# Within-chunk decays of an SSD scan on Trainium2: ten-row matmuls of split running sums in place of masked 128-row matmuls

## The chip, the cores and the metric

The kernel runs as one program on one core of a Trainium2 chip. The metric is the device time of one execution in microseconds (us). The core has a matrix engine (TensorE, in the profile PE; its weight loads are shown apart as PEld), a vector engine (VectorE, DVE), a scalar engine (ScalarE, ACT), GpSimd (POOL) and SyncE (SP). Each runs its own instructions in a fixed order; semaphores make one engine wait for another. Matmuls write to PSUM, a small memory of banks of 128 x 512 fp32 numbers; everything else stands in SBUF, both with 128 partitions.

## The reference, cut to what matters

The network has two layers on 512 latent tokens (and 256 context tokens) of width 1024. The change is in layer 0, in the Mamba-2 state-space scan (SSD) with 16 heads of width 64 in 2 groups, run once forward and once backward (d = 0, 1), in chunks of 128 tokens:

```python
def ssd_scan(xs, dt, a_coef, bm, cm, h0):
    xdt = (xs * dt[..., None])
    a = dt * a_coef                          # a_coef < 0, per head
    a_cum = jnp.cumsum(a, -1)                # within a chunk
    decay = jnp.exp(segsum(a))               # exp(a_cum[t] - a_cum[s]) for s <= t, else 0
    cb = jnp.einsum('bclgn,bcsgn->bgcls', cc, bc)
    y_diag = jnp.einsum('bgcls,bgjcls,bcsgjp->bclgjp', cb, decay, xdt)
    # ... plus what comes over from earlier chunks (y_off), by exp(a_cum)
```

So for each of 4 chunks, 16 heads and both directions a 128 x 128 table of exponents is needed, which for source token s and target token t holds the difference of two running sums; its exponential, times dt of the source and times `cb`, is the weight with which the source's 64 values go into the target's output. The forward tables are zero for s > t, the backward ones for s < t. A skip term adds `ssd_d` times the input.

## The kernel before, in words

`mixer` (L350 ff.) projects layer 0's input. PE does the projections with weights split in a high and a low fp32r part: per block of 128 input channels three matmuls (L214 to L216) of 512 columns (latents, tile `ps`) or 256 (context, also `ps`). A weight block comes from memory as `wraw`, is cast on ScalarE to `whi` (L184), and VectorE or POOL makes `wlo` as the difference (L188). Few such blocks are in SBUF at a time, so a cast also waits until PE has finished with an older block. The results of a projection for the SSD go through a five-tap convolution, `conv5`: ScalarE does the middle tap from PSUM (L332), VectorE adds four taps, also from PSUM (L336), ScalarE applies silu (L339); PE transposes the result (L347, `pt`) and ScalarE copies it out (L348). The projections' PSUM pool `mm` has four banks; a fifth projection waits until the taps of the first have read its bank. Pools `lv` and `mi` have two banks each.

`dt_stage` (L512) computes dt and a = -dt x exp(a_log) for all chunks, heads and directions (VectorE, up to L552), then with six matmuls `p` (L560 to L562) against triangles of ones the running sums and totals; ScalarE takes their exponentials, `ef` and `dtot` (L565, L566), which free the two `mi` banks, and VectorE makes `wdec`.

`ssd` (L592) is called for the two groups of 8 heads, g = 0 and 1. It makes the states that chunks hand on (matmuls `u`, L620 to L624 and L675) and `pcb`, the products of B and C for four chunks (L629); two VectorE products give `cbm`, masked for forward and backward (L633). Then for each of 4 chunks and for each half `hq` of the group's heads (four heads; 16 such half-chunks in both groups):

- ScalarE multiplies a triangle of ones by `a`, per head and direction: 8 tiles `r` of 128 x 128 (L644)
- PE multiplies these with the strict triangle, one fp32 matmul `seg` of 512 columns a direction, both accumulated in one `lv` bank (L645): the exponents of both directions, each zero where the other counts
- ScalarE takes the exponential to `e` (L647, the one reader of the bank)
- ScalarE and VectorE make `w`, the masked `cbm` times dt of either direction (L650, L651, four each)
- VectorE multiplies `e` by `w` (L653), and PE uses each head's part as the stationary operand of a matmul `yp` (L656).

After each chunk come the two inter-chunk terms `po` (L661), the skip product and the sums on VectorE (L663 to L671, the last is `y` times the gate `sz`) and a square on ScalarE with a running sum (L672).

Between these, PE works on the next weight matmuls: for g = 0 on group 1's projections, for g = 1 on the `v` projection of the gla heads that come next (tile `psv`, copied out by ScalarE at L496) and on the first gla gates (`ps`, L697). The first matmul of a gla head that depends on all of this is `lev` (L733). The order on each engine isn't that of the source: the build lays the whole program out by its dependencies, and the result is a fixed list for each engine.

Of the kernel before, what the change touches and what calls it, by code (L numbers as in the profile page):

```python
# [8 lines left out]
F32 = mybir.dt.float32  # L9
F32R = mybir.dt.float32r  # L10
BF16 = mybir.dt.bfloat16
I32 = mybir.dt.int32
AF = mybir.ActivationFunctionType
ALU = mybir.AluOpType
# [3 lines left out]
P = 128  # L18
D = 1024
KT = D // P  # L20
T = 512
TC = 256
NCH = T // P
# [115 lines left out]
def ap(t, off, dims):  # L139
    a = t[:]  # L140
    return bass.AP(tensor=a.tensor, offset=a.offset + off, ap=[list(a.ap[0])] + [list(d) for d in dims])
# [6 lines left out]
class Net:  # L148
# [201 lines left out]
    def mixer(self):  # L350
# [93 lines left out]
        sp = ss.enter_context(self.pool("ssp", 1))  # L444
        dx = self.stack()
# [3 lines left out]
        dt, a, ef, dtot, wdec = dts  # L449
        self.dump("dt", dt)  # L450
# [61 lines left out]
    def dt_stage(self, act, actc, sp, sx, mm, mi, rows):  # L512
# [51 lines left out]
        dtot = sp.tile([P, 2, NC6, H], F32, name="dtot")  # L564
        nc.scalar.activation(out=ef, in_=p1, func=AF.Exp)  # L565
# [6 lines left out]
        return dt, a, ef, dtot, wdec  # L572
# [19 lines left out]
    def ssd(self, g, y, xct, bfm, cfm, btok, dts, rows, sz, sp, tmps, lv, mi):  # L592
        nc = self.nc
        dt, a, ef, dtot, wdec = dts
# [4 lines left out]
        def bch(t, n):  # L599
            return bass.AP(tensor=t.tensor, offset=t.offset, ap=[list(t.ap[0]), [1, t.shape[1]], [0, n]])  # L600
# [29 lines left out]
        cbm = sp.tile([P, 2, NCH, P], F32, tag="cbm", name="cbm")  # L630
        for d in range(2):
            m = (self.le, self.ge)[d]
            nc.vector.tensor_tensor(out=cbm[:, d], in0=pcb, in1=bass.AP(tensor=m.tensor, offset=m.offset, ap=[list(m.ap[0]), [0, NCH], [1, P]]), op=ALU.mult)  # L633
        ssq = tmps.tile([P, NCH], F32, tag="ssq", name="ssq")
        for c in range(NCH):
            yp = mi.tile([P, 512], F32, tag="mi", name="yp")
            for hq in range(2):
                h0 = g * GH + hq * 4
                r = tmps.tile([P, 2, 4, P], F32, tag="r", name="r", bufs=1)
                seg = lv.tile([P, 4, P], F32, tag="lv", name="seg")  # L640
                for d in range(2):
                    m = (self.le, self.ge)[d]
                    for j in range(4):
                        nc.scalar.mul(r[:, d, j, :], m, a[:, c, d, h0 + j:h0 + j + 1])  # L644
                    nc.tensor.matmul(seg, (self.gt, self.lt)[d], r[:, d], start=d == 0, stop=d == 1)  # L645
                e = tmps.tile([P, 4, P], F32, tag="e", name="e")
                nc.scalar.activation(out=e, in_=seg, func=AF.Exp)  # L647
                w = tmps.tile([P, 4, P], F32, tag="w", name="w")
                for j in range(4):
                    nc.scalar.mul(w[:, j, :], cbm[:, 1, c, :], dt[:, c, 1, h0 + j:h0 + j + 1])  # L650
                    nc.vector.scalar_tensor_tensor(out=w[:, j, :], in0=cbm[:, 0, c, :], scalar=dt[:, c, 0, h0 + j:h0 + j + 1],  # L651
                                                   in1=w[:, j, :], op0=ALU.mult, op1=ALU.add)
                nc.vector.tensor_tensor(out=e, in0=e, in1=w, op=ALU.mult)  # L653
                for j in range(4):
                    hh = hq * 4 + j
                    nc.tensor.matmul(yp[:, hh * HD:(hh + 1) * HD], e[:, j, :], y[:, c, (g * GH + hh) * HD:(g * GH + hh + 1) * HD], start=True, stop=True)  # L656
# [9 lines left out]
            dd = rows[:, R_D - R_DTB + g * GH:R_D - R_DTB + (g + 1) * GH]  # L666
            nc.vector.tensor_tensor(out=heads(yc), in0=heads(yc), in1=bch(dd, HD), op=ALU.mult)
# [577 lines left out]
def layout(inp):  # L1245
# [25 lines left out]
    out["tri"] = np.concatenate([(s == t), (s <= t), (s >= t), (s > t), (s < t)], 1).astype(np.float32)  # L1271
    out["msk"] = np.concatenate([((s // m) ^ (t // m)) == 1 for m in (1, 2, 4, 8, 16, 32, 64)], 1).astype(np.int32)
# [16 lines left out]
```

## Time and profile before

| | us |
|---|---|
| median of 3 runs | 1736.62 |
| lowest, highest | 1735.19, 1737.04 |
| the profiled execution | 1734.44 |
| its span, first to last instruction | 1732.7 |
| PE busy in it | 1696.8 |
| DVE busy | 1220.2 |
| ACT busy | 849.9 |
| POOL busy | 520.0 |

The profile is of one execution. In its rows a line such as `L645 PE MATMUL seg<-r,tri 128x512 x64` names the line of the code, the engine, the operation, the tile written and those read, the form and the count; an fp32 matmul counts as two records. `[0.46 <-DVE y L671]` behind a row is idle time of the engine ahead of it and what ended it. The mean granted clock of TensorE was 0.994 of the full one.

### The profile page before, as it was taken

How to read it: one execution, taken by the hardware profiler on the slowest of the kernel's cores; microseconds unless marked ns; L12 is line 12 of the kernel's file. 1: busy time of each engine (PE TensorE's matmuls, PEld its weight loads, DVE VectorE, ACT ScalarE, POOL GpSimd, SP SyncE). 2: the span in 40 equal slices, each digit the busy share in tenths (PEclk: the TensorE clock that was granted, in tenths of full speed). 3: DMA queues.
4: the chain of work that ended last, by engine and by line, in shares of the span. 5: the costliest groups of instructions: out<-in, count | busy, mean ns of one | idle time of the engine just before them, and what ended most of it. 6: DMA issues, size and time to landing. Idle time of an engine off the chain costs nothing.

```text
span 1732.7 us, 26538 instructions
## 1 busy us (share of the span) xinstructions
PE 1696.8 (98%) x9574; PEld 1458.9 (84%) x9574; DVE 1220.2 (70%) x2416; ACT 849.9 (49%) x1718; POOL 520.0 (30%) x434
## 2 busy tenths in 40 slices
PE   7999999999999999999999999999999999999997
PEld 5987778989999898898888888988899888888886
DVE  7778987979696894768777741378887876666114
ACT  4556775344444553365333332499635743333223
POOL 4400000000000000545444454533424444444443
PEclk9999999999999999999999999999999999999998
DMA  9721002444344233834334343422213333333332
GB/s 362 244 73 50 29 22 90 135 145 147 132 150 139 92 122 102 263 92 130 109 109 121 109 134 97 113 77 55 62 31 86 97 93 97 97 98 97 98 98 79
DMA packets 92195, 194.03 MB, mean 112 GB/s; under 512 B 10496, under 2 KB 13568, under 8 KB 92064
## 3 DMA queue, kind: packets, MB, share of 16 engines
q1 hardware_dynamic: 92016, 192.21, 36.2%
q8 instruction: 75, 1.23, 0.3%
q14 instruction: 56, 0.46, 0.1%
q0 software_dynamic: 48, 0.13, 0.0%
HBM read 190.21 MB, written 2.10 MB: 111 GB/s over the span
## 4 chain that ended last, share of the span: by engine, by line
PE 93%; DVE 3%; ACT 1%; issue 0%; POOL 0%; ACTq 0%; POOLq 0%; DVEq 0%
PE ps L214 18%; PE ps L216 18%; PE ps L215 18%; PE lev L744 3%; PE psg L215 2%; PE psg L216 2%; PE psg L214 2%; PE psh L214 2%; PE psh L215 2%; PE psh L216 2%; PE psz L235 2%; PE psz L234 2%; PE psz L233 2%; PE seg L645 2%; PE psv L234 1%; PE psv L235 1%
## 5 line engine op out<-in xcount | busy, mean ns | idle before, releaser
L188 POOL TENSOR_TENSOR wlo<-wraw,whi 128x512 fp32r<-128x512 f32 x380 | 499.9, 1319 | 1171.7 <-ACT whi L184 1154.7
L184 ACT CAST whi<-wraw 128x512 fp32r<-128x512 f32 x488 | 300.7, 619 | 501.6 <-PE ps L215 249.1
L214 PE MATMUL ps<-h1hi,whi 128*128 128x512 f32 x768 | 299.1, 389 | 0.8 <-DVE acc L1105 0.8
L216 PE MATMUL ps<-h1hi,wlo 128*128 128x512 f32 x768 | 299.0, 389 | 0.2 <-POOL wlo L188 0.2
L215 PE MATMUL ps<-h1lo,whi 128*128 128x512 f32 x768 | 298.9, 389 | 0.0
L1105 DVE SCALAR_TENSOR_TENSOR acc<-ps,pcol,acc 128x441 f32<-128x441 f32 (+2 forms) x320 | 222.4, 695 | 56.9 <-ACT acc L1097 47.4
L214 PEld LDWEIGHTS ps<-h1hi,whi 128*128 128x128 f32 x768 | 144.2, 188 | 30.8 <-issue 1.6
L216 PEld LDWEIGHTS ps<-h1hi,wlo 128*128 128x128 f32 x768 | 144.2, 188 | 30.4 <-POOL wlo L188 0.6
L215 PEld LDWEIGHTS ps<-h1lo,whi 128*128 128x128 f32 x768 | 144.2, 188 | 29.4
L273 DVE CUSTOM_DVE_ANT_0 junk<-ada,sc,pcol 128x1024 bf16<-128x1024 f32 x80 | 106.4, 1330 | 8.7 <-DMA ada<-adaw 8.4
L909 DVE SCALAR_TENSOR_TENSOR x<-ps,mod,x 128x512 f32<-128x512 f32 x14 | 10.5, 750 | 139.0 <-PE ps L216 139.0
L188 DVE TENSOR_TENSOR wlo<-wraw,whi 128x512 fp32r<-128x512 f32 x108 | 73.9, 691 | 42.4 <-ACT whi L184 42.1
L214 PE MATMUL ps<-ghi,whi 128*128 128x512 f32 x264 | 102.7, 389 | 0.0
L215 PE MATMUL ps<-glo,whi 128*128 128x512 f32 x264 | 102.7, 389 | 0.0
L216 PE MATMUL ps<-ghi,wlo 128*128 128x512 f32 x264 | 102.7, 389 | 0.0
L1197 DVE SCALAR_TENSOR_TENSOR cr<-u,pcol,cr 128x511 f32<-128x511 f32 (+20 forms) x156 | 97.9, 702 | 1.4 <-ACT cr L1180 1.2
L214 PE MATMUL ps<-hhi,whi 128*128 128x512 f32 x240 | 97.9, 408 | 0.0
L215 PE MATMUL ps<-hlo,whi 128*128 128x512 f32 x240 | 96.7, 403 | 0.0
L216 PE MATMUL ps<-hhi,wlo 128*128 128x512 f32 x240 | 96.2, 401 | 0.0
L1016 DVE TENSOR_TENSOR glo<-acc,ghi 128x512 fp32r<-128x512 f32 x44 | 56.0, 1273 | 28.2 <-ACT ghi L1015 28.0
L233 PE MATMUL psz<-whi,hhi 128*128 128x256 f32 (+1 forms) x224 | 67.6, 302 | 0.0
L234 PE MATMUL psz<-wlo,hhi 128*128 128x256 f32 (+1 forms) x224 | 67.4, 301 | 0.0
(361 smaller groups left out, 4122.8 us busy)
## 6 DMA issues: line engine op xcount, KB each, us to landing
wraw<-wst SPq DMA_DIRECT2D x488, 256.0 KB, 2.7
ada<-adaw SPq DMA_DIRECT2D x104, 512.0 KB, 3.6
xk<-xT SPq DMA_DIRECT2D x8, 256.0 KB, 7.8
x<-xT SPq DMA_DIRECT2D x8, 256.0 KB, 5.3
out<-n SPq DMA_DIRECT2D x16, 128.0 KB, 1.7
xk<-ctxT SPq DMA_DIRECT2D x8, 128.0 KB, 3.7
sc<-rows SPq DMA_DIRECT2D x1, 512.0 KB, 3.6
scc<-rows SPq DMA_DIRECT2D x1, 512.0 KB, 7.6
```

The lines of the kernel that those rows point to most:

```text
L184: nc.scalar.copy(hi, raw)
L188: eng.tensor_tensor(out=lo, in0=raw, in1=hi.bitcast(F32), op=ALU.subtract)
L214: mm(ps, w[0], a[0], start=start, stop=False)
L215: mm(ps, w[0], a[1], start=False, stop=False)
L216: mm(ps, w[1], a[0], start=False, stop=stop)
L233: mm(ps, a[0], w[0], start=start, stop=False)
L234: mm(ps, a[0], w[1], start=False, stop=False)
L235: mm(ps, a[1], w[0], start=False, stop=stop)
L273: nc.vector.tensor_tensor_reduce(out=junk, in0=raw, in1=self.sc if cond is None else cond, scale=1.0, scalar=self.pc("adab", n), op0=ALU.m ...
L1016: return nc.vector.tensor_tensor(out=lo, in0=x, in1=hi.bitcast(F32), op=ALU.subtract)
L1105: nc.vector.scalar_tensor_tensor(out=o, in0=grid(pg)[:, r0 + dy - 1:r1 + dy - 1, c0 + dx - 1:c1 + dx - 1], scalar=wcol(dy, dx), in1=o, op0 ...
L1197: nc.vector.scalar_tensor_tensor(out=acc[:, t0:t1], in0=u[:, t0 + d:t1 + d], scalar=self.pc("cdw", tap * 8 + i), in1=acc[:, t0:t1], op0=AL ...
```

## The change

The exponents are computed from the running sums themselves. In `dt_stage` the sums of both directions (`cum`, copied from the `p` bank) and ln(dt) - cum (`nb`: a maximum, ScalarE's Ln, a difference; rearranged as `nbt`) are transposed by eight PE transposes `pr` to rows of 512 tokens, each split in a high and a low fp32r part (`crow`: a ScalarE cast and a VectorE difference), and written to a DRAM tile by a DMA on POOL's queue. Per group and chunk, two more DMAs on POOL's queue bring ten rows each: `etgt`, of which two rows are the target's split sums and eight are the marks of the four heads (ones in that head's 128 columns), and `esrc`, two rows of ones and eight rows of the source's split constants of four heads. One ten-row fp32r matmul of 512 columns then gives the exponents of four heads and one direction, with ln(dt) inside. The marks and ones are laid down once by four memsets and four DMAs on POOL's queue.

Per half-chunk there are now two such `seg`, one for each direction, in a bank each, so one half-chunk uses both banks of `lv`. ScalarE copies the forward one to `e`, VectorE lays the backward one over it where the source comes after the target (a copy under a mask), ScalarE takes the exponential in SBUF, and VectorE multiplies by `cb`, which a ScalarE copy takes from `pcb` once per group. The tiles `r`, `w` and `cbm` go. On the diagonal, where both directions count, only the forward one is left by this; so per group and chunk VectorE takes the diagonal of `cb` (a product with the identity and its sum), multiplies it by the backward dt and adds it to the skip factor: `own`, which takes the place of that factor in the skip product.

```diff
@@ -442,12 +442,19 @@
         mi = psx.enter_context(self.pool("mi", 2, PSUM))
 
         sp = ss.enter_context(self.pool("ssp", 1))
+        self.cumd = ss.enter_context(self.pool("cumd", 1, bass.MemoryType.DRAM)).tile([4, 2 * H, T], F32R, name="cumd")
+
+
+        self.esrc = sp.tile([P, 4, P], F32R, name="esrc")
+        self.etgt = sp.tile([P, 4, 4 * P], F32R, name="etgt")
+        for c in range(NCH):
+            nc.gpsimd.memset(self.esrc[32 * c:32 * c + 2].bitcast(F32), 1.0)
+            nc.gpsimd.dma_start(out=self.etgt[32 * c + 2:32 * c + 10].rearrange("p x t -> p (x t)"), in_=A["ind"].bitcast(F32R))
         dx = self.stack()
         dts = self.dt_stage(act, actc, sp, dx.enter_context(self.pool("dtx", 1)), mm, mi, rows)
         dx.close()
         tmps = ss.enter_context(self.pool("sst", 2))
-        dt, a, ef, dtot, wdec = dts
-        self.dump("dt", dt)
+        self.dump("dt", dts[0])
 
         for g in range(2):
             ps = mm.tile([P, TC], F32, tag="mm", name="ps")
@@ -562,6 +569,27 @@
             nc.tensor.matmul(p2[:, d], self.ones, ad, start=True, stop=True)
         ef = sp.tile([P, 4, NC6, H], F32, name="ef")
         dtot = sp.tile([P, 2, NC6, H], F32, name="dtot")
+
+        cum = sx.tile([P, NCH, H // 4, 2, 4], F32, name="cum")
+        by4 = lambda t: t.rearrange("p c (q j) -> p c q j", j=4)
+        for d in range(2):
+            nc.vector.tensor_copy(cum[:, :, :, d, :], by4(p1[:, d, 0:NCH, :]))
+
+        nb = sx.tile([P, NCH, 2, H], F32, name="nb")
+        nc.vector.tensor_scalar_max(nb, dt[:, 0:NCH], 1e-30)
+        nc.scalar.activation(out=nb, in_=nb, func=AF.Ln)
+        for d in range(2):
+            nc.vector.tensor_tensor(out=by4(nb[:, :, d, :]), in0=by4(nb[:, :, d, :]), in1=cum[:, :, :, d, :], op=ALU.subtract)
+        nbt = sx.tile([P, NCH, 4, H // 4, 2], F32, name="nbt")
+        for d in range(2):
+            nc.vector.tensor_copy(nbt[:, :, :, :, d].rearrange("p c j q -> p c q j"), by4(nb[:, :, d, :]))
+        crow = sx.tile([2 * H, 4, T], F32R, name="crow")
+        for i, t in enumerate((cum, nbt)):
+            pr = mi.tile([P, T], F32, tag="mi", name="pr")
+            for c in range(NCH):
+                nc.tensor.transpose(pr[:2 * H, c * P:(c + 1) * P], t[:, c].rearrange("p x y z -> p (x y z)"), self.ident)
+            self.split(pr[:2 * H, :], crow[:, 2 * i, :], crow[:, 2 * i + 1, :])
+        nc.gpsimd.dma_start(out=self.cumd[:].rearrange("k r t -> r k t"), in_=crow)
         nc.scalar.activation(out=ef, in_=p1, func=AF.Exp)
         nc.scalar.activation(out=dtot, in_=p2, func=AF.Exp)
         wdec = sp.tile([P, 2, NC6, H], F32, name="wdec")
@@ -569,7 +597,7 @@
             nc.vector.tensor_tensor(out=wdec[:, d], in0=ef[:, 2 + d], in1=dt[:, :, d, :], op=ALU.mult)
         for d, c, c2 in ((0, NCH, NCH + 1), (1, NCH + 1, NCH)):
             nc.vector.tensor_tensor(out=wdec[:, d, c, :], in0=wdec[:, d, c, :], in1=dtot[:, d, c2, :], op=ALU.mult)
-        return dt, a, ef, dtot, wdec
+        return dt, ef, dtot, wdec
 
     def zproj(self, i, sz, acth, pool, tag, col=C_Z, dst=None):
 
@@ -591,7 +619,7 @@
 
     def ssd(self, g, y, xct, bfm, cfm, btok, dts, rows, sz, sp, tmps, lv, mi):
         nc = self.nc
-        dt, a, ef, dtot, wdec = dts
+        dt, ef, dtot, wdec = dts
         NC6 = NCH + NCC
         ch = lambda t, d, c: t[:, d, c, g * GH:(g + 1) * GH]
         heads = lambda t: t.rearrange("p (h d) -> p h d", h=GH)
@@ -627,30 +655,40 @@
         pcb = lv.tile([P, NCH, P], F32, tag="lv", name="pcb")
         for c in range(NCH):
             nc.tensor.matmul(pcb[:, c, :], bfm[:, g, c * P:(c + 1) * P], cfm[:, g, c * P:(c + 1) * P], start=True, stop=True)
-        cbm = sp.tile([P, 2, NCH, P], F32, tag="cbm", name="cbm")
-        for d in range(2):
-            m = (self.le, self.ge)[d]
-            nc.vector.tensor_tensor(out=cbm[:, d], in0=pcb, in1=bass.AP(tensor=m.tensor, offset=m.offset, ap=[list(m.ap[0]), [0, NCH], [1, P]]), op=ALU.mult)
+        cb = sp.tile([P, NCH, P], F32, tag="cb", name="cb")
+        nc.scalar.copy(cb, pcb)
+
+        own = sp.tile([P, NCH, GH], F32, tag="own", name="own")
+        cbd = sp.tile([P, NCH], F32, tag="cbd", name="cbd")
+        dd = rows[:, R_D - R_DTB + g * GH:R_D - R_DTB + (g + 1) * GH]
+        for c in range(NCH):
+            junk = tmps.tile([P, P], F32, tag="cj", name="cj", bufs=1)
+            nc.vector.tensor_tensor_reduce(out=junk, in0=cb[:, c, :], in1=self.ident, scale=1.0, scalar=0.0, op0=ALU.mult, op1=ALU.add,
+                                           accum_out=cbd[:, c:c + 1])
+            nc.vector.scalar_tensor_tensor(out=own[:, c, :], in0=dt[:, c, 1, g * GH:(g + 1) * GH], scalar=cbd[:, c:c + 1], in1=dd,
+                                           op0=ALU.mult, op1=ALU.add)
+        after = bass.AP(tensor=self.gt.tensor, offset=self.gt.offset, ap=[list(self.gt.ap[0]), [0, 4], [1, P]]).bitcast(I32)
+        for c in range(NCH):
+            tok = slice(c * P, (c + 1) * P)
+            nc.gpsimd.dma_start(out=self.etgt[32 * c:32 * c + 2].rearrange("p x (j t) -> p (x j) t", j=4), in_=self.cumd[0:2, g * 16:(g + 1) * 16, tok])
+            nc.gpsimd.dma_start(out=self.esrc[32 * c + 2:32 * c + 10],
+                                in_=self.cumd[2:4].rearrange("k (j x) t -> (k j) x t", j=4)[:, g * 4:(g + 1) * 4, tok])
         ssq = tmps.tile([P, NCH], F32, tag="ssq", name="ssq")
         for c in range(NCH):
             yp = mi.tile([P, 512], F32, tag="mi", name="yp")
             for hq in range(2):
-                h0 = g * GH + hq * 4
-                r = tmps.tile([P, 2, 4, P], F32, tag="r", name="r", bufs=1)
-                seg = lv.tile([P, 4, P], F32, tag="lv", name="seg")
+
+                e = tmps.tile([P, 4, P], F32, tag="e", name="e")
+                segs = []
                 for d in range(2):
-                    m = (self.le, self.ge)[d]
-                    for j in range(4):
-                        nc.scalar.mul(r[:, d, j, :], m, a[:, c, d, h0 + j:h0 + j + 1])
-                    nc.tensor.matmul(seg, (self.gt, self.lt)[d], r[:, d], start=d == 0, stop=d == 1)
-                e = tmps.tile([P, 4, P], F32, tag="e", name="e")
-                nc.scalar.activation(out=e, in_=seg, func=AF.Exp)
-                w = tmps.tile([P, 4, P], F32, tag="w", name="w")
-                for j in range(4):
-                    nc.scalar.mul(w[:, j, :], cbm[:, 1, c, :], dt[:, c, 1, h0 + j:h0 + j + 1])
-                    nc.vector.scalar_tensor_tensor(out=w[:, j, :], in0=cbm[:, 0, c, :], scalar=dt[:, c, 0, h0 + j:h0 + j + 1],
-                                                   in1=w[:, j, :], op0=ALU.mult, op1=ALU.add)
-                nc.vector.tensor_tensor(out=e, in0=e, in1=w, op=ALU.mult)
+                    seg = lv.tile([P, 4, P], F32, tag="lv", name="seg")
+                    rows10 = slice(32 * c, 32 * c + 10)
+                    nc.tensor.matmul(seg, self.esrc[rows10, hq * 2 + d, :], self.etgt[rows10, hq * 2 + d, :], start=True, stop=True)
+                    segs.append(seg)
+                nc.scalar.copy(e, segs[0])
+                nc.vector.copy_predicated(e, after, segs[1])
+                nc.scalar.activation(out=e, in_=e, func=AF.Exp)
+                nc.vector.tensor_tensor(out=e, in0=e, in1=ap(cb, c * P, [[0, 4], [1, P]]), op=ALU.mult)
                 for j in range(4):
                     hh = hq * 4 + j
                     nc.tensor.matmul(yp[:, hh * HD:(hh + 1) * HD], e[:, j, :], y[:, c, (g * GH + hh) * HD:(g * GH + hh + 1) * HD], start=True, stop=True)
@@ -663,8 +701,7 @@
                 nc.vector.tensor_tensor(out=heads(t[:]), in0=heads(po[:]), in1=bch(ch(ef, d, c), HD), op=ALU.mult)
                 offs.append(t)
             yc = y[:, c, g * 512:(g + 1) * 512]
-            dd = rows[:, R_D - R_DTB + g * GH:R_D - R_DTB + (g + 1) * GH]
-            nc.vector.tensor_tensor(out=heads(yc), in0=heads(yc), in1=bch(dd, HD), op=ALU.mult)
+            nc.vector.tensor_tensor(out=heads(yc), in0=heads(yc), in1=bch(own[:, c, :], HD), op=ALU.mult)
             nc.vector.tensor_tensor(out=yc, in0=yc, in1=yp, op=ALU.add)
             nc.vector.tensor_tensor(out=offs[0], in0=offs[0], in1=offs[1], op=ALU.add)
             nc.vector.tensor_tensor(out=yc, in0=yc, in1=offs[0], op=ALU.add)
@@ -1269,6 +1306,8 @@
     out["rows"] = np.concatenate([f["c"][0], f["c_ctx"], f["ssd_dt_bias"][0].ravel(), f["ssd_a_log"][0].ravel(), f["ssd_d"][0]])[None]
     s, t = np.arange(P)[:, None], np.arange(P)[None, :]
     out["tri"] = np.concatenate([(s == t), (s <= t), (s >= t), (s > t), (s < t)], 1).astype(np.float32)
+    j = np.arange(8)[:, None, None, None] % 4
+    out["ind"] = np.broadcast_to(j == np.arange(4)[None, None, :, None], (8, 4, 4, P)).astype(np.float32).reshape(8, 16 * P)
     out["msk"] = np.concatenate([((s // m) ^ (t // m)) == 1 for m in (1, 2, 4, 8, 16, 32, 64)], 1).astype(np.int32)
     return out
```

How the instructions now stand is shown at three places.

ScalarE at the dt stage, before. `whi` are the weight casts, `cacc` the first steps of two B convolutions on the context and of those on the latents, `ef` and `dtot` the exponentials:

```order
L184 CAST whi_1237<-wraw_1235 128x512
L332 ACTIVATE cacc<-ps,pcol 128x256 x2
L332 ACTIVATE cacc<-bfm,pcol 128x512
L565 ACTIVATE ef<-p_1095 128x384
L566 ACTIVATE dtot<-p_1096 128x192
L332 ACTIVATE cacc<-cfm,pcol 128x512
L184 CAST whi_1243<-wraw_1241 128x512
L644 ACTIVATE r<-tri,a 128x128 x2
L184 CAST whi_1323<-wraw_1321 128x512
L339 ACT_TABLE_LOAD
```

The same place now:

```order
L184 CAST whi_1277<-wraw_1275 128x512
L580 ACT_TABLE_LOAD
L580 ACTIVATE nb<-nb 128x128
L594 ACT_TABLE_LOAD
L594 ACTIVATE dtot<-p_1109 128x192
L593 ACTIVATE ef<-p_1108 128x384
L1052 CAST crow<-pr 32x512 x2
L184 CAST whi_1283<-wraw_1281 128x512
L184 CAST whi_1363<-wraw_1361 128x512
L332 ACTIVATE cacc<-ps,pcol 128x256 x2
L332 ACTIVATE cacc<-bfm,pcol 128x512
L332 ACTIVATE cacc<-cfm,pcol 128x512
```

The Ln, a table load, `dtot`, `ef`, the two `crow` casts and two weight casts now stand ahead of the first steps of the B convolutions, which stood ahead of `ef` before.

PE in the first of the two SSD loops (`seg` the exponents, `yp` and `po` the chunk's output terms, `u` a state, `ps` the projections of the other group), before:

```order
L656 MATMUL yp<-y,e 128x64 x4
L645 MATMUL seg<-r,tri 128x512
L661 MATMUL po<-sf,cfm 128x512
L645 MATMUL seg<-r,tri 128x512
L214 MATMUL ps<-hhi,whi_1579 128x512
L215 MATMUL ps<-hlo,whi_1579 128x512
L216 MATMUL ps<-hhi,wlo_1581 128x512
L214 MATMUL ps<-hhi,whi_1579 128x512
L661 MATMUL po<-sb,cfm 128x512
L215 MATMUL ps<-hlo,whi_1579 128x512
L656 MATMUL yp<-y,e 128x64 x4
L645 MATMUL seg<-r,tri 128x512
```

and now:

```order
L694 MATMUL yp<-y,e 128x64 x4
L699 MATMUL po<-sf,cfm 128x512
L694 MATMUL yp<-y,e 128x64 x4
L686 MATMUL seg<-etgt,esrc 128x512 x2
L214 MATMUL ps_2040<-chi,whi_1541 128x256
L215 MATMUL ps_2040<-clo,whi_1541 128x256
L216 MATMUL ps_2040<-chi,wlo_1543 128x256
L214 MATMUL ps_2040<-chi,whi_1541 128x256
L699 MATMUL po<-sb,cfm 128x512
L686 MATMUL seg<-etgt,esrc 128x512
L215 MATMUL ps_2040<-clo,whi_1541 128x256
L216 MATMUL ps_2040<-chi,wlo_1543 128x256
```

The two `seg` of a half-chunk stood apart with other matmuls between, both going to one bank; now they follow each other or nearly so, each to its own bank.

ScalarE at the end of the second loop (`yo,ssq` is the square of a chunk's output, `v` the three copies that free banks of `psv`), before:

```order
L672 ACTIVATE yo,ssq<-y 128x512
L647 ACTIVATE e<-seg 128x512
L184 CAST whi_2847<-wraw_2845 128x512
L184 CAST whi_2853<-wraw_2851 128x512
L184 CAST whi_2859<-wraw_2857 128x512
L184 CAST whi_3021<-wraw_3019 128x512
L672 ACTIVATE yo,ssq<-y 128x512
L496 COPY v<-psv 128x512 x3
```

and now:

```order
L688 COPY e<-seg 128x512
L184 CAST whi_2864<-wraw_2862 128x512
L690 ACTIVATE e<-e 128x512
L709 ACTIVATE yo,ssq<-y 128x512
L690 ACTIVATE e<-e 128x512
L709 ACTIVATE yo,ssq<-y 128x512
L503 COPY v<-psv 128x512 x3
```

In both lists the three `v` copies stand behind the last square; the weight casts that stood ahead of it have moved forward, and two exponentials stand there instead.

## Prediction

> **What bounds the kernel now.** I read the page's busy shares first, then windows around the changed stage, then the chain of waits, then groups and timelines. The page says which engine sets the time:
>
> ```profile
> PE 1696.8 (98%) x9574; PEld 1458.9 (84%) x9574; DVE 1220.2 (70%) x2416; ACT 849.9 (49%) x1718; POOL 520.0 (30%) x434
> ```
>
> That is a mean over the span. The changed code runs between about 105 and 298 us; the windows there (span, then busy us and count of PE, PEld, DVE, ACT and POOL, the clock, the DMA share, GB/s) read:
>
> ```profile
> 160.00:170.00 10.00, 10.00 (x40) 5.92 (x39) 9.14 (x19) 5.80 (x19) 0.00 (x0) 1.00 0.00 1
> 180.00:190.00 10.00, 10.00 (x53) 7.04 (x52) 9.43 (x23) 9.95 (x30) 0.00 (x0) 1.00 0.05 7
> ```
>
> PE is full, but VectorE stands at 91 to 94%: it is the next bound, close behind. In the chain of waits, the first work beyond the change is the `lev` matmul of the first gla head:
>
> ```profile
> 294.84 0.23 PE ps L216
> 297.94 0.89 PE lev L733 x8
> ```
>
> From there on the orders of PE, VectorE and ScalarE are the same in both kernels, so what this matmul gains or loses is the change of the whole time. The sum runs from the end of the dt stage's last `p` matmul, about 106.9, to this one: 297.94 - 106.9 = 191.0 us.
>
> **PE's own work in the 191.0 us.** PE's price of an instruction is the distance between starts; the recorded duration overlaps its neighbours. The timeline has start, duration and form (an fp32 matmul of 512 columns is two records):
>
> ```profile
> 109.31 0.28 PE L214 MATMUL ps<-chi,whi 128*128 128x256 f32 x1
> 109.43 0.28 PE L215 MATMUL ps<-clo,whi 128*128 128x256 f32 x1
> ...
> 113.21 0.40 PE L214 MATMUL ps<-hhi,whi 128*128 128x512 f32 x1
> 113.44 0.39 PE L215 MATMUL ps<-hlo,whi 128*128 128x512 f32 x1
> ...
> 119.33 1.05 PE L629 MATMUL pcb<-cfm,bfm 128*128 128x128 f32 x8
> 120.22 1.02 PE L645 MATMUL seg<-r,tri 128*128 128x512 f32 x2
> ...
> 121.78 0.82 PE L347 MATMUL pt<-tri,cacc 128*128 128x128 f32 x6
> 122.35 0.48 PE L214 MATMUL ps<-hhi,whi 128*128 128x512 f32 x1
> ```
>
> ```profile
> 154.94 1.02 PE L645 MATMUL seg<-r,tri 128*128 128x512 f32 x2
> 155.80 1.02 PE L620 MATMUL u<-xd,btok 128*128 128x512 f32 x2
> ```
>
> ```profile
> 276.04 0.84 PE yp L656 x8
> ```
>
> So split (fp32r) matmuls cost 0.12 us at 256 columns and 0.23 at 512; a transpose (121.78 to 122.35, six) 0.095; a `pcb` matmul 0.22; `seg` 0.86; a head's `yp` 0.21. The order has between the two ends 479 of 256 columns (57.5 us), 216 of 512 (49.4), 60 transposes (5.7), 36 `u`/`po` at seg's price (31.0), 8 `pcb` (1.8), 64 `yp` (13.4) and 32 `seg` (27.5): 186.3 us. The remaining 4.7 us of the 191.0 are waits and changes of form.
>
> Removed: 32 `seg` go from 0.86 to 0.23, as the ten-row operands are fp32r of 512 columns: 32 x 0.63 = -20.2 us. If ten rows ran at the old 0.86, nothing would go. Added: eight transposes `pr`, 8 x 0.095 = +0.8. PE's work becomes 166.9 us. What counts is how much of that 19.4 us PE can use.
>
> **Place A, the dt stage: a conv is held up.** These timeline rows set the times before, VectorE first, then ScalarE, which waits 4.73 us for `p`:
>
> ```profile
> 105.00 0.36 DVE L552 SCALAR_TENSOR_TENSOR a<-dt,ea 128x192 f32<-128x192 f32 x1
> 105.28 1.65 DVE L336 SCALAR_TENSOR_TENSOR cacc<-ps,pcol,cacc 128x254 f32<-128x254 f32 x4
> ```
>
> ```profile
> 100.88 0.55 ACT L332 ACTIVATE cacc<-ps,pcol 128x256 f32<-128x256 f32 x1
> ...
> 106.87 0.49 ACT L565 ACTIVATE ef<-p 128x384 f32<-128x384 f32 x1 [4.73 <-PE p L561]
> 107.26 0.33 ACT L566 ACTIVATE dtot<-p 128x192 f32<-128x192 f32 x1
> ...
> 109.75 0.62 ACT L184 CAST whi<-wraw 128x512 fp32r<-128x512 f32 x1 [0.18 <-PE ps L215]
> 110.39 1.28 ACT L339 ACT_TABLE_LOAD   x1
> ```
>
> Before, the taps of the B convolution (L336) start at 105.28, their first ScalarE step long done. In the new order ScalarE does first: `nb`'s Ln, a table load back to Exp (1.28), `dtot`, `ef`, two `crow` casts, and the weight casts `whi_1283` and `whi_1363`, and only then that first step. `whi_1363` needs a weight buffer that PE frees with its last 256-column matmul of this `ps`. PE is done with it at about 109.6 before (one step after 109.43); now the transposes add 0.8 and wait 0.3 (Ln ends at about 105.9, the table load at 107.2, `dtot` at 107.5, `ef` at 107.9; only these free the PSUM banks of `pr`): about 110.65. A cast of 0.6 and a tap step of 0.5 later VectorE does one `wlo` and starts the taps at about 111.9. Two convs alternate, eight taps at 0.41 (1.65 / 4); the seventh is the first conv's last, so its bank is read out at about 115.0. PE's next matmul group writes that bank: it waits 110.65 to 115.0 = 4.35. Behind it the transposes of these conv results wait for the silu, which reloads its table (1.28), and for the B latents: about 1.7. With the 0.3, place A costs 6.4 us. If the taps weren't last, the rest would be some 2 us; if the Ln or the casts run longer, A grows by as much.
>
> The transfers are free. POOL computes nothing here (0.00 in both windows above), and its one DMA before shows the price of an issue and of a landing:
>
> ```profile
> L516 POOL DMA_DIRECT2D wd<-wdt x1: 703/703/703, 78.4 to 78.4; - x1
> ```
>
> ```profile
> wd<-wdt POOLq DMA_DIRECT2D x1, 128.0 KB, 4.7
> ```
>
> The write of `crow`, issued near 110, lands at about 115.5; eight row loads follow, 8 x 0.7 + 4.7, and are in by 126. The first `seg` comes after 155. The second group's loads have the whole first loop. The four mask loads stand earlier on POOL's queue, between its weight subtractions; I take them as covered, and uncovered they cost at most 4 x 0.7 = 2.8.
>
> **Places B and C, the two loops: VectorE.** The groups (busy us, mean ns; then what its engine waited):
>
> ```profile
> L651 DVE SCALAR_TENSOR_TENSOR w<-cbm,dt,w 128x128 f32<-128x128 f32 x64 | 20.0, 346 | 2.8 <-ACT w L650 2.8
> L653 DVE TENSOR_TENSOR e<-e,w 128x512 f32<-128x512 f32 x16 | 11.0, 687 | 0.6 <-ACT e L647 0.2
> L633 DVE TENSOR_TENSOR cbm<-pcb,tri 128x512 f32<-128x512 f32 x4 | 2.6, 681 | 0.0
> L644 ACT ACTIVATE r<-tri,a 128x128 f32<-128x128 f32 x128 | 39.5, 390 | 0.0
> ```
>
> ```profile
> L746 DVE COPY_PREDICATED p<-msk,lev x56: 725/741/757, 300.7 to 625.6; 128x512 f32<-128x512 int32 x56
> L734 ACT COPY p<-lev x8: 586/587/589, 298.9 to 602.7; 128x512 f32<-128x512 f32 x8
> ```
>
> The overlay has a twin in the trace: same size, PSUM data, an integer mask, 741 ns. Neighbours on VectorE overlap by about 80 ns (685 ns operations stand 605 apart), so I count 0.66 for it, 0.605 for `cbm`, 0.26 for `w`. Out: 64 x 0.26 + 4 x 0.605 = 19.1. In: 16 x 0.66 = 10.6, and eight diagonals (product with sum, read of the sum, `own`), 0.46 each by the 346 ns row plus two short ones, 3.7. VectorE sheds 4.8 us here, PE 20.2. ScalarE sheds 39.5 (`r`) and 20.6 (`w`), against 32 copies and exps of some 0.59: it is no bound.
>
> A VectorE that was 91 to 94% busy and sheds 4.8 us can't follow a PE that sheds 20.2. Laying the new order out by these durations, PE waits about 1.0 for `e` and banks in the first loop and 2.55 for a bank that a conv tap frees behind VectorE's backlog (B: 3.5). In the second loop it waits 0.5, and at its end 4.7: PE's `ps` for the gla gates needs a bank that the `v` copies free, and these stand on ScalarE behind the last square, which waits for VectorE's last `y`. Before, that pair had cover:
>
> ```profile
> 282.38 0.63 ACT L672 ACTIVATE yo<-y 128x512 f32<-128x512 f32 x1 [0.46 <-DVE y L671]
> ...
> 283.01 1.54 ACT L496 COPY v<-psv 128x512 f32<-128x512 f32 x3
> ```
>
> ```profile
> 286.56 0.28 PE L214 MATMUL ps<-chi,whi 128*128 128x256 f32 x1
> ```
>
> The copies begin 3.5 us before the bank is wanted; the cover goes as PE pulls ahead. A late `wlo` adds 1.45 (C: 6.6 in all).
>
> **The clock.** Two of these waits exceed 4 us, and short PE gaps show what follows:
>
> ```profile
> 768.00:769.00 1.00, 0.15 (x2) 0.00 (x0) 0.78 (x3) 0.00 (x0) 0.00 (x0) 1.00 0.00 0
> 769.00:770.00 1.00, 0.25 (x2) 0.25 (x3) 0.97 (x4) 0.90 (x2) 0.00 (x0) 1.00 0.00 0
> ...
> 771.00:772.00 1.00, 1.00 (x9) 1.00 (x7) 1.00 (x4) 1.00 (x3) 0.00 (x0) 0.68 0.00 0
> 772.00:773.00 1.00, 1.00 (x6) 1.00 (x6) 0.71 (x3) 1.00 (x3) 0.00 (x0) 0.50 0.03 8
> 773.00:774.00 1.00, 1.00 (x7) 1.00 (x7) 0.93 (x3) 1.00 (x4) 0.00 (x0) 0.50 0.00 0
> 774.00:775.00 1.00, 1.00 (x7) 1.00 (x7) 1.00 (x4) 0.58 (x2) 0.84 (x1) 0.61 0.00 0
> ```
>
> After 1.6 us without work in two, the clock fell: 0.32 + 0.50 + 0.50 + 0.39 = 1.7 us lost. Two drops are 3.4 us, but the waits right behind (1.7 in A, 1.45 in C) absorb most, as PE then reaches late data later: 0.3 to 3.4, I take 0.8. The Trainium skill, "TensorE: Matmul & The Clock Gate" (Why this matters for your kernels), warns of PE-idle gaps over about 3 us between bursts; by that rule both waits would be hit, and the time would be that of the clock rival below. The row agrees, and already at a shorter gap.
>
> **The sum.** Work 166.9, waits 6.4 + 3.5 + 6.6 = 16.5, clock 0.8, and of the old 4.7 us about 0.6 for changes of form (the rest were waits, counted anew): 184.8, against 191.0: -6.2 us. The profiled execution took 1734.44, so 1728.2 in its terms; the median of the three runs lies 2.18 higher: **1730.4 us**.
>
> **Rivals.** A measurement of this kernel can tell about 0.2%, 3.5 us, from no change.
> - *The saving comes whole.* PE has 19.4 us less to do, and the waits at A and C are mostly an artefact of my layout: 7.5 us are left of 16.5 (A's 2, B, and 2 at C), and no clock drop. 166.9 + 7.5 + 0.6 = 175.0, so -16.0: 1720.6. For it: ScalarE loses 60 us of work. Against: the casts ahead of the conv's first step are in the order, and VectorE's 94%. Chance 0.13.
> - *A wash.* Every half-chunk's chain (two `seg`, copy, overlay, exp, product) changes engine four times, where before it was two; each turn a little later than I count, 0.3 us for each of 16 half-chunks, is 4.8: 1735.2. The gain falls under 3.5 us from 0.17 each. Chance 0.16.
> - *The clock in full.* Both drops cost their 1.7 with nothing absorbed: 2.6 more than I take, 1733.0, at the edge of what can be told; with drops at the shorter waits too it lies beyond. For: the row above needed only 1.6 us. Chance 0.06.
> - *Slower.* The same chain binds: both `lv` banks now belong to one half-chunk, so the next `seg` stands in PE's queue behind the copy (0.59) and the overlay (0.74), and all later matmuls behind it. If PE waits 1.0 us more in each half-chunk: 16 - 6.2 = +9.8, 1746.4. It decides from 0.39 us each, and is slower by over 3.5 from 0.61. For: VectorE's 94%, so overlays queue. Against: in the order, weight matmuls stand between most pairs. Chance 0.11.
> - *The change doesn't do what it says:* ten-row matmuls at 0.86. The saving is gone, and of the waits, about 10 us go as PE comes later: -6.2 + 20.2 - 10 = +4.0, 1740.6. The fp32r rows at 0.23 speak against it. Chance 0.04.
>
> **How the numbers follow.** The forecast has 0.50: gain of 3.5 to 10, 1726 to 1733. Faster: 0.50 + 0.13 = 0.63; same 0.16 + 0.06 = 0.22; slower 0.11 + 0.04 = 0.15. The range 1720 to 1739 leaves out half of the first rival (0.06) and most of the slower ones (0.13).
>
> **What would show it.** After: `seg` spaced 0.23 on PE; first `lev` at about 291.7; a PE wait over 4 us near 111 ended by a conv tap, one of 4 to 5 near 274 ended by the `v` copies; VectorE over 92% between 160 and 280. Wrong if PE stays full there (first rival), or if waits gather at `seg` and `yp` (the others).

## The result, and the profile after

The change makes the kernel slower: 1745.26 us (median of 4 runs, 1744.69 to 1746.87) against 1735.9 (1734.15 to 1737.04) in the same comparison, a ratio of 1.0055 with a 95% interval of 1.0043 to 1.0068. That is 9.4 us more, where 6.2 less were forecast. The profiled execution has a span of 1744.0 us.

The page's busy shares and the windows of the stage (columns as in the prediction):

```profile
PE 1694.1 (97%) x9550; PEld 1456.0 (83%) x9550; DVE 1215.7 (70%) x2397; ACT 807.5 (46%) x1547; POOL 533.5 (31%) x459
```

```profile
160.00:170.00 10.00, 9.90 (x32) 4.59 (x30) 9.31 (x21) 4.21 (x8) 0.00 (x0) 1.00 0.33 103
180.00:190.00 10.00, 10.00 (x51) 6.53 (x50) 7.41 (x13) 3.75 (x9) 1.07 (x2) 1.00 0.04 5
210.00:220.00 10.00, 7.82 (x30) 5.80 (x29) 9.66 (x22) 4.11 (x7) 0.00 (x0) 0.70 0.22 57
260.00:270.00 10.00, 10.00 (x56) 6.83 (x54) 7.97 (x13) 3.62 (x7) 0.00 (x0) 1.00 0.01 2
290.00:300.00 10.00, 5.33 (x27) 4.66 (x26) 8.67 (x25) 5.20 (x10) 0.00 (x0) 0.83 0.62 203
```

The whole stretch from 160 to 280 us, before and then now:

```profile
160.00:280.00 120.00, 119.94 (x606) 85.40 (x605) 107.22 (x220) 86.36 (x238) 0.00 (x0) 1.00 0.07 18
160.00:280.00 120.00, 117.70 (x590) 83.09 (x589) 99.89 (x197) 49.03 (x89) 4.53 (x8) 0.97 0.10 28
```

In the windows from 180 and from 260 us PE is still full, and VectorE stands at 74 and 80%; over the whole stretch it has fallen from 89 to 83%, where over 92% was foreseen. In the loops it is mostly PE that is late, not VectorE. In two of the five windows PE stands and the clock is below 1. The list of PE's waits gives their releasers (total us, times, longest), and the chain of waits the end of the stage:

```profile
PE ps L214 <- DVE cacc L336: 6.2, 2, 4.1
PE ps L214 <- ACT v L503: 4.7, 1, 4.7
```

```profile
293.27 0.70 DVE y L708
294.78 0.48 ACT v L503
308.26 0.89 PE lev L770 x8
```

The waits are those of the forecast: at a conv tap in the dt stage (4.1 us, forecast 4.35), at a tap in the first loop (2.1; 2.55), at the `v` copies (4.7; 4.7). In the chain the `v` copies follow VectorE's last `y`, as foreseen. Yet `lev` comes at 308.26, where it stood at 297.94. The `p` matmuls already start later, at 106.84 against 105.51 (in the runs below this start lies anywhere from 105.73 to 107.38); from the last `p` to `lev` it is 200.1 us, against 191.0 before and 184.8 forecast.

So 15.3 us are missing in the forecast of this stretch. The distances between PE's starts show the greater part. The timeline of the change, around a lone `seg` in the first loop and around one in the second:

```profile
172.34 0.39 PE L216 MATMUL ps<-hhi,wlo 128*128 128x512 f32 x1
172.66 0.49 PE L686 MATMUL seg<-etgt,esrc 10*128 10x512 f32 x1
173.07 0.50 PE L214 MATMUL ps<-hhi,whi 128*128 128x512 f32 x1
173.41 0.39 PE L215 MATMUL ps<-hlo,whi 128*128 128x512 f32 x1
...
261.93 0.28 PE L233 MATMUL psv<-whi,hhi 128*128 128x256 f32 x1
262.14 0.50 PE L686 MATMUL seg<-etgt,esrc 10*128 10x512 f32 x1
262.57 0.39 PE L234 MATMUL psv<-wlo,hhi 128*128 128x256 f32 x1
262.79 0.28 PE L235 MATMUL psv<-whi,hlo 128*128 128x256 f32 x1
```

From 172.34 to 173.41 stand three matmuls of 512 columns, which at 0.23 would take 0.69; they take 1.07. From 261.93 to 262.79, with two of 256 columns, it is 0.86 and not 0.47. So one ten-row `seg` among matmuls of 128 rows costs 0.23 and about 0.38 beside it: the matmul ahead of it takes 0.09 longer, it itself 0.19, the one behind it 0.10. Two `seg` in a row pay it once. PE makes 28 such visits for its 32 `seg`: 28 x 0.38 = 10.6 us.

The kernel before holds a hint of this price, two small transposes `ptd` of 32 rows, just ahead of the stage that was read:

```profile
93.83 0.29 PE L216 MATMUL ps<-chi,wlo 128*128 128x256 f32 x1
94.05 0.31 PE L529 MATMUL ptd<-tri,dfm 32*128 32x32 f32 x2
94.28 0.39 PE L214 MATMUL ps<-chi,whi 128*128 128x256 f32 x1
94.51 0.28 PE L215 MATMUL ps<-clo,whi 128*128 128x256 f32 x1
```

The matmuls ahead of and behind them take 0.22 and 0.23 in place of 0.12, much as beside `seg`. It is a hint only, since six transposes of 128 rows also leave the 512-column matmul behind them 0.09 longer (122.35 to 122.67), though not the one ahead (121.54 to 121.78).

The next part is the clock. The windows of 1 us at the dt stage's wait and behind it:

```profile
114.00:115.00 1.00, 0.00 (x0) 0.00 (x0) 1.00 (x3) 1.00 (x2) 0.01 (x1) 1.00 0.82 283
115.00:116.00 1.00, 0.00 (x0) 0.00 (x0) 1.00 (x4) 0.18 (x1) 1.00 (x2) 0.51 0.70 182
...
120.00:121.00 1.00, 1.00 (x4) 0.80 (x3) 1.00 (x3) 0.07 (x1) 0.00 (x0) 0.50 0.23 32
121.00:122.00 1.00, 1.00 (x4) 0.77 (x3) 1.00 (x3) 0.63 (x1) 0.00 (x0) 0.58 0.00 0
```

The clock falls at about 115.0, while PE still waits. PE resumes at 116.45 and runs at half clock until about 121.8: some 2.7 us lost by the granted clock. The same comes with the other two waits (the means 0.70 and 0.83 above), about 2.9 and 1.7. Gross that is 7.3 us, where 0.8 was taken.

Two more terms of the sum were off, in opposite directions. The waits were put at 16.5 us, and the three that the list shows are 10.9. And of the 4.7 us that the kernel before spends beyond its counted work, the sum kept 0.6 and took the rest for waits. The window of nearly the whole stretch before shows next to none:

```profile
107.00:297.00 190.00, 189.82 (x1030) 144.89 (x1030) 164.54 (x334) 134.47 (x337) 0.00 (x0) 1.00 0.15 45
```

PE stands 0.2 us of 190 there, so most of the 4.7 isn't waiting and stays (changes of form, and prices a little too low: which, isn't shown). Work 166.9, visits 10.6, waits 10.9, clock 7.3 and these 4.7 make 200.4, against the 200.1 measured.

### The profile page after: what moved, and what is told of

Same layout as the page of the kernel before. It is cut to its first block, busy times and chain, and to the rows that moved or that the text cites. A ratio compares the mean times of both kernels' runs of the same rounds, so it can differ in the third digit from the quotient of the medians.

```text
span 1744.0 us, 26353 instructions
## 1 busy us (share of the span) xinstructions
PE 1694.1 (97%) x9550; PEld 1456.0 (83%) x9550; DVE 1215.7 (70%) x2397; ACT 807.5 (46%) x1547; POOL 533.5 (31%) x459
## 4 chain that ended last, share of the span: by engine, by line
PE 91%; DVE 4%; ACT 1%; issue 0%; POOL 0%; ACTq 0%; POOLq 0%; DVEq 0%
PE ps L214 18%; PE ps L215 18%; PE ps L216 18%; PE lev L781 3%; PE psg L215 2%; PE psh L214 2%; PE psh L215 2%; PE psh L216 2%; PE psg L216 2%; PE psg L214 2%; PE psz L234 2%; PE psz L235 2%; PE psz L233 2%; PE psv L234 1%; PE psv L235 1%; PE psv L233 1%
```

## The experiments

Each kernel was timed beside the kernel before on the same chip. The first four undo or isolate one part. A difference from the change is one of medians from two comparisons; the kernel before stood between 1735.9 and 1736.8 in them.

**e1, `seg` over 128 rows.** The source tile gets a slice for each chunk, zero outside its ten rows, so a matmul over all partitions gives the same sums:

```diff
-        self.esrc = sp.tile([P, 4, P], F32R, name="esrc")
+        self.esrc = sp.tile([P, NCH, 4, P], F32R, name="esrc")
...
+        nc.gpsimd.memset(self.esrc[:].bitcast(F32), 0.0)
+        nc.gpsimd.memset(self.etgt[:].bitcast(F32), 0.0)
...
-                    nc.tensor.matmul(seg, self.esrc[rows10, hq * 2 + d, :], self.etgt[rows10, hq * 2 + d, :], start=True, stop=True)
+                    nc.tensor.matmul(seg, self.esrc[:, c, hq * 2 + d, :], self.etgt[:, hq * 2 + d, :], start=True, stop=True)
```

> The exponents are the same, but each seg matmul now runs over all 128 rows: the source tile is zero outside the chunk's ten rows. Two memsets are added on POOL. In the first loop PE's order is that of the changed kernel; in the second some seg stand later, since a load of the target rows now waits for all seg of the first loop. Theory 1 (the visit price): a ten-row matmul between 128-row ones costs PE about 0.39 us beyond its own 0.23, 28 visits, 10.8 us. Then a lone seg's three distances (before it, its own, behind it) add up to 0.58 among 256-column matmuls and not to 0.82, PE loses about 10 us of work, and the time falls by 4 to 10 us, to 1735 to 1741. Theory 2 (the price is the change of banks: seg waits for the copy and the overlay): the distances stay and so does the time, 1743 to 1747.

Measured: 1735.91 us, ratio to the kernel before 0.9997 (0.9988 to 1.0007); 9.4 us less than the change. The timeline, a `seg` in each loop:

```profile
170.04 0.39 PE L216 MATMUL ps<-hhi,wlo 128*128 128x512 f32 x1
170.28 0.39 PE L687 MATMUL seg<-etgt,esrc 128*128 128x512 f32 x1
170.50 0.39 PE L214 MATMUL ps<-hhi,whi 128*128 128x512 f32 x1
...
263.42 0.28 PE L235 MATMUL psv<-whi,clo 128*128 128x256 f32 x1
263.53 0.40 PE L687 MATMUL seg<-etgt,esrc 128*128 128x512 f32 x1
263.77 0.28 PE L233 MATMUL psv<-whi,chi 128*128 128x256 f32 x1
263.88 0.28 PE L234 MATMUL psv<-wlo,chi 128*128 128x256 f32 x1
```

Now `seg` takes 0.22 to 0.24, and its neighbours 0.24, 0.11 and 0.11: no price for the visit. More rows, all of them zero, make the matmul cheaper here. Theory 1 holds, in the distances and in the sum. Change of banks, which is the same in this kernel, isn't the cause. PE's waits for taps and `v` copies hardly change in sum (10.9 to 10.9), so the gain isn't theirs; the drops of the clock in this trace are shorter than in the change's (about 1.7 us lost each), and how much of the 9.4 that gives the medians don't tell.

**e2, the rows made later.** The sums are copied out of PSUM in the dt stage; the Ln, the transposes, the splits and the write move behind the second convolution group of group 0.

```diff
...
+                if g == 0 and i == 2:
+                    self.crow_stage(tmps, mi)
                 ps, ps2 = self.fm(mm, "win", C_XS + (g * 4 + i) * P, act, also=actc)
```

> The Ln, the transposes, the splits and the write of the rows are moved in the program to behind the second convolution group of group 0 (four DMA writes in place of one); the same is computed. On ScalarE the first steps of the B convolutions stand ahead of ef again. Theory 1 (place A costs a 4.1 us wait and the clock drop behind it, 5.5 us at half speed): the wait at 112 to 116 us and the half clock behind it go, and the time falls by 5 to 8 us, to 1737 to 1740. Theory 2 (what is won here is given back at the next wait, since VectorE sets the pace): the wait goes, those at 213 and 291 us grow by as much, and the time stays within 2 us of 1745.

Measured: 1737.81 us, ratio 1.0007 (0.9997 to 1.0016); 7.5 us less than the change. PE's waits in it:

```profile
PE ps L214 <- ACT v L506: 4.3, 1, 4.3
PE pt L347 <- ACT cacc L339: 1.2, 1, 1.2
PE seg L696 <- ACT e L698: 0.7, 1, 0.7
PE seg L696 <- ACT cb L669: 0.5, 1, 0.5
```

The wait for a conv tap is gone, and the one at the end hasn't grown. Theory 1. But the wait of 2.1 us for a tap in the first loop is gone too (a drop of the clock still comes there, at 206 us), so the 7.5 us aren't the price of place A alone.

**e3, the kernel before with the dt stage of the change alone.** The rows are made and written, and nobody reads them.

```diff
+        cum = sx.tile([P, NCH, H // 4, 2, 4], F32, name="cum")
...
+        nc.gpsimd.dma_start(out=self.cumd[:].rearrange("k r t -> r k t"), in_=crow)
         nc.scalar.activation(out=ef, in_=p1, func=AF.Exp)
```

> The kernel before with the dt stage of the change alone: running sums, Ln, transposes, splits and the DRAM write are made, and nobody reads them; the loops are those of before. Theory 1: the wait at about 112 us and its clock drop come alone, and the time rises by 5 to 9 us over before, to 1741 to 1745. Theory 2 (the dt stage is harmless and the loops make the kernel slower): the time is within 2 us of before, 1734 to 1738.

Measured: 1745.92 us, ratio 1.0055 (1.004 to 1.007): 9.3 us more than before, as much as the whole change. So in the change the two loops together won and lost nothing, to within some 2 us: what the cheaper `seg` saved went to waits and drops of the clock. Its one long wait:

```profile
PE ps L214 <- DVE cacc L336: 4.1, 1, 4.1
```

**e4, the last square on VectorE.** ScalarE's `v` copies no longer stand behind an instruction that waits for VectorE.

```diff
-            nc.scalar.activation(out=offs[1], in_=yc, func=AF.Square, accum_out=ssq[:, c:c + 1])
+            if g == 1 and c == NCH - 1:
+                nc.vector.tensor_tensor_reduce(out=offs[1], in0=yc, in1=yc, scale=1.0, scalar=0.0, op0=ALU.mult, op1=ALU.add, accum_out=ssq[:, c:c + 1])
+            else:
+                nc.scalar.activation(out=offs[1], in_=yc, func=AF.Square, accum_out=ssq[:, c:c + 1])
```

> The last chunk's square and sum of group 1 are made by VectorE, behind its last product, so that the copies of v on ScalarE no longer stand behind an instruction that waits for VectorE; PE's order is unchanged. Theory 1 (the 4.7 us wait at 291 us is ScalarE's order): the wait shrinks below 1 us, the clock drop behind it goes, and the time falls by 4 to 7 us, to 1738 to 1741. Theory 2 (VectorE sets the pace there anyway): PE waits as long for a weight part or a gate further on, and the time stays within 2 us of 1745.

Measured: 1740.29 us, ratio 1.0018 (1.0008 to 1.0028); 5.0 us less than the change. The wait:

```profile
PE ps L214 <- ACT v L503: 0.4, 1, 0.4
```

It shrank by 4.3 us, and the clock behind it stayed whole. Theory 1.

**e6, `seg` over 32 rows.** As the change, with the 22 rows below the ten zeroed.

```diff
...
-                    rows10 = slice(32 * c, 32 * c + 10)
+                    rows10 = slice(32 * c, 32 * c + 32)
```

> As the changed kernel, but each seg runs over 32 rows, the 22 below the ten being zero; order unchanged, two memsets added on POOL. Theory 1a (any matmul of fewer than 128 rows pays on entering and leaving): distances of a lone seg as with ten rows, 0.42 for its own, time 1743 to 1747. Theory 1b (only a row count that isn't a multiple of 32 pays): 0.23 and 1735 to 1741, as with 128 rows.

Measured: 1744.42 us, ratio 1.0043 (1.0028 to 1.0057). The timeline:

```profile
170.51 0.39 PE L216 MATMUL ps<-hhi,wlo 128*128 128x512 f32 x1
170.83 0.49 PE L688 MATMUL seg<-etgt,esrc 32*128 32x512 f32 x1
171.25 0.50 PE L214 MATMUL ps<-hhi,whi 128*128 128x512 f32 x1
171.59 0.39 PE L215 MATMUL ps<-hlo,whi 128*128 128x512 f32 x1
```

The distances 0.32, 0.42 and 0.34 are those of ten rows. Theory 1a: what PE pays for is going from 128 rows to 32 or fewer and back, not the odd count. (64 rows weren't tried.) In this trace the wait of 2.1 us in the first loop has no drop of the clock behind it.

**e7, the wait filled.** As the change, with 16 matmuls nobody reads, in PE's list just at the dt stage's wait.

```diff
+                    warm = lv.tile([P, T], F32, tag="lv", name="warm")
+                    for j in range(16):
+                        nc.tensor.matmul(warm, self.wtiles[34][0][:, 0:P], act(0)[0], start=True, stop=True)
```

> As the changed kernel, with 16 extra fp32r matmuls of 512 columns (16 x 0.23 = 3.7 us) on PE just where it waits 4.1 us at 112 us, into a free bank that nobody reads; nothing else moves. Theory 1 (half of place A's price is the clock): the clock stays at 1.00 from 115 to 122 us, and the time falls by 1.5 to 3 us, to 1742.3 to 1743.8, although there is more work. Theory 2 (the waits behind absorb the drop, as the prediction took it): the time stays within 1 us of 1745.3 or rises.

Measured: 1743.11 us, ratio 1.0039 (1.0025 to 1.0052); 2.15 us less than the change, with more work on PE. Timeline, windows and waits:

```profile
111.95 3.81 PE L475 MATMUL warm<-hhi,whi 128*128 128x512 f32 x16
116.25 0.47 PE L214 MATMUL ps<-hhi,whi 128*128 128x512 f32 x1 [0.49 <-DVE cacc L336]
```

```profile
117.00:118.00 1.00, 0.47 (x3) 0.05 (x1) 1.00 (x3) 0.99 (x3) 1.00 (x3) 1.00 0.28 27
118.00:119.00 1.00, 1.00 (x7) 0.81 (x8) 1.00 (x2) 0.78 (x3) 1.00 (x3) 1.00 0.29 26
```

```profile
PE pt L347 <- ACT cacc L339: 0.5, 1, 0.5
PE pt L347 <- ACT bfm L339: 0.4, 1, 0.4
```

PE resumes at 116.25 (its `p` started 0.2 earlier too), and the clock is whole. At whole speed PE comes to the transposes `pt` too early and waits 0.9 us for them; in the change these two waits don't appear, as the slow clock covers them. So they absorb 0.9 of the drop, a third. When the second of these `pt` starts, this run is 1.3 us ahead (121.84 against 123.16), at the end 2.15 by the medians: the drop at this one wait costs the kernel 1 to 2 us net. Theory 1.

**e5 and e9, the edits together.** e5 is e1, e2 and e4 in one kernel, e9 only e1 and e2.

```diff
+        nc.gpsimd.memset(self.esrc[:].bitcast(F32), 0.0)
...
+                    self.crow_stage(tmps, mi)
...
+                nc.vector.tensor_tensor_reduce(out=offs[1], in0=yc, in1=yc, scale=1.0, scalar=0.0, op0=ALU.mult, op1=ALU.add, accum_out=ssq[:, c:c + 1])
```

> The seg over all 128 rows, the rows made behind the second convolution group, and the last square on VectorE, together. Theory 1 (three separate prices): the savings of the single edits, 9.4 + 7.5 + 5.0 us against the changed kernel, add up to some 22 us, 1723 us, that is 13 us under the kernel before. Theory 2 (VectorE is the bound once PE has room, as the prediction had it): the savings overlap, VectorE is over 92% busy from 160 to 280 us, and the time stays at 1728 to 1734.

> The seg over 128 rows and the rows made later, without the square on VectorE. Theory 1 (the wait at the end of the second loop keeps its own price): 1728.4 + 5 = 1733. Theory 2 (with place A's and the visits' price gone, this wait is no longer the last): 1728 to 1730.

Measured: e5 1728.39 us, ratio 0.9951 (0.9938 to 0.9963): faster than both kernels. e9 1733.86, ratio 0.9985 (0.9975 to 0.9994). The wait at the second loop's end keeps its price, 5.5 us between the two. But e5 is 5 us above the sum of the single savings. Its longest wait, and the window:

```profile
PE ps L214 <- DVE cacc L336: 3.3, 1, 3.3
```

```profile
200.00:210.00 10.00, 6.70 (x22) 4.88 (x21) 10.00 (x29) 4.90 (x9) 0.00 (x0) 0.66 0.16 52
```

With PE relieved, VectorE is now full there, and PE waits for its conv tap 3.3 us where it was 2.1; the clock falls again. Over 160 to 280 us, though, VectorE is busy for 105.31 us, 88% and not 92. Part of theory 2, then: its time, at the lower edge, and one place where VectorE binds.

**e8, a sum moved to GpSimd.** As e5, and:

```diff
-            nc.vector.tensor_tensor(out=offs[0], in0=offs[0], in1=offs[1], op=ALU.add)
+            nc.gpsimd.tensor_tensor(out=offs[0], in0=offs[0], in1=offs[1], op=ALU.add)
```

> The three edits together, and the sum of a chunk's two inter-chunk terms made by GpSimd in place of VectorE (8 of 0.69 us off VectorE; GpSimd takes about 1.3 us each). PE's order in the loops moves a little with it. Theory 1 (VectorE sets the pace in what is left): the 3.3 us wait for a conv tap at 200 us shrinks, and the time falls by another 2 to 5 us, to 1723.5 to 1726.5. Theory 2 (what is left is not VectorE's, or GpSimd's slower sum takes its place): within 1 us of 1728.4, or above.

Measured: 1721.78 us, ratio 0.9914 (0.9897 to 0.993), the fastest of all; 6.6 us less than e5, more than expected. The sum by itself and the waits left:

```profile
L717 POOL TENSOR_TENSOR yo<-yo x8: 1267/1288/1773, 171.9 to 269.0; 128x512 f32<-128x512 f32 x8
```

```profile
PE ps L214 <- DVE cacc L336: 1.2, 1, 1.2
PE pt L347 <- ACT cacc L339: 1.2, 1, 1.2
PE yp L705 <- DVE e L702: 1.0, 2, 0.6
```

GpSimd takes 1.29 us for what VectorE did in 0.69, and the time falls all the same. The order moved with the edit, so the 6.6 us aren't the sum's price alone; the wait is down to 1.2, and no drop of the clock follows it:

```profile
200.00:210.00 10.00, 8.77 (x52) 7.29 (x51) 10.00 (x28) 6.27 (x12) 1.88 (x3) 1.00 0.22 57
```

**e10, the control.** The kernel before with the edit of e8 alone (L669):

```diff
-            nc.vector.tensor_tensor(out=offs[0], in0=offs[0], in1=offs[1], op=ALU.add)
+            nc.gpsimd.tensor_tensor(out=offs[0], in0=offs[0], in1=offs[1], op=ALU.add)
```

> A control: the kernel before, with only the sum of the two inter-chunk terms on GpSimd. Theory 1 (before the change PE is the bound, so relief of VectorE is worth nothing there): within 2 us of before. Theory 2 (the relief helps whatever PE does, and e8's last gain isn't owed to the room on PE): faster by 4 to 7 us, as in e8.

Measured: 1738.68 us, ratio 1.0012 (1.0002 to 1.0021), 2.0 us more, at the edge of theory 1's band and against theory 2: where PE is the bound, relief of VectorE gives nothing.

## Why the prediction was wrong, point by point

- *What bounds the kernel: right.* PE was the bound, and nearly the whole change was settled ahead of the first `lev` (10.3 us there, 11.3 in the whole span of the two traces). That VectorE can't follow was wrong for the change, where PE stayed the late one; it showed only in e5 and e8, with PE relieved. The 91 to 94% were two windows; over 160 to 280 us VectorE stood at 89% before.
- *The step that failed:* "Removed: 32 `seg` go from 0.86 to 0.23, as the ten-row operands are fp32r of 512 columns". The price was read from matmuls of 128 rows. With 28 visits a `seg` costs 0.23 + 28/32 x 0.38 = 0.56: a saving of about 9.6 us, not 20.2. The cost had to be bounded from both sides, and the only bound given, 0.86, was handed to a rival with 0.04. The trace of before had a hint in its `ptd`, shown above. The Trainium skill has a rule that speaks against the step, "TensorEngine Tiling (Array Packing)" (Key Properties): changing the tiling mode drains TensorE. The runs fit it, with 0.38 us a visit for 10 and 32 rows and none for 128 (e1, e6); that the ten-row `seg` is such a change of mode isn't shown by them.
- *A second term mis-sized:* "of the old 4.7 us about 0.6 for changes of form (the rest were waits, counted anew)". PE waited 0.2 us in that stretch before, so nearly all of the 4.7 stayed. The waits, put at 16.5, were 10.9, which more than makes up for it: the small ones of the sum (4.9 us beside the three large) don't show in the list.
- *Place A: right in kind and place, too small.* The wait came as worked out (4.1 for 4.35), behind the casts and ahead of the taps. With its transposes it was to cost 7.2 us; e3 measured 9.3, and e7 gives 1 to 2 of that to the clock.
- *The clock: the direction right, the size wrong.* The bounds 0.3 to 3.4 held two drops of 1.7. There were three, two of them twice as long as the one they were taken from, at 1.7 to 2.9 gross; and the waits behind place A absorb 0.9 us (e7), not most of it. The rule cited there held for the two waits above 4 us; the wait of 2.1 us in the first loop was followed by a drop too, though not in the trace of e6.
- *Places B and C: right in their main waits.* 2.1 for 2.55, 4.7 for 4.7 with VectorE's last `y` ahead of it; e4 prices C with its drop at 5.0.
- *The rivals.* The time came to that of the slower rival, 1746.4, but not by its mechanism: e1 keeps the hand-over of the `lv` banks and loses the 9.4 us. What happened is half of "the change doesn't do what it says", between 0.23 and 0.86 a `seg`, together with "the clock in full", which had named drops at the shorter waits too. The 0.15 for slower was too little.

The loss so has three prices, each undone alone: the visits 9.4 us, place A 7.5, the end of the second loop 5.0. They overlap in part: all three undone give 16.9. (The 7.5 hold the wait of 2.1 us in the first loop as well.)

## What to carry to other kernels

A matmul of few rows isn't priced by its columns alone: read the distances of its neighbours too, and if it stands alone among matmuls of 128 rows, fill it up with zero rows. Where PE is the bound, look at what a new step is placed ahead of on the other engines: here a wait of 2 to 5 us mostly cost another 1.6 to 3.1 us gross by the clock. And when PE sheds work, look for the next engine at once: with its three prices undone and VectorE relieved, the same change is 14.8 us faster than the kernel before (e8).

## What the runs showed of the hardware

- A lone `seg` of 10 or 32 rows among matmuls of 128 takes 0.42 us from its start to the next, the matmuls ahead of and behind it 0.09 and 0.10 more; of 128 rows 0.23 and nothing more. A second one directly behind adds 0.24.
- Each drop to half clock in this stretch lasted 3.4 or 6.8 us (twice the sum of 1 minus the granted clock over its windows: from 115 to 122 us 0.49 + 5 x 0.50 + 0.42 = 3.41, so 6.8), and the same wait had one or the other, or none, in different runs: at the 4.1 us wait 6.8 (the change, e3, e4) and 3.4 (e1, e6), at the 2.1 us wait 6.8 (the change, e4), 3.4 (e7) and none (e6). The one shown in the prediction lasted 3.4. A drop in one trace is thus no measure of its mean price.
- GpSimd's sum of 128 x 512 beside a busy VectorE took 1.29 us (median), as its `wlo` differences do (1.30).
